# A planner inside a kernel gets a limit of eight transfers in flight, a price for results read on their own engine, later landings, and twelve rounds

## The chip, the core and the metric

The kernel runs on one core of one Trainium2 chip. The metric is the device time of one execution in microseconds; the median of several runs counts.

## The reference

One decoder layer, float32, on 2048 tokens of width 1024. The input projection feeds two groups side by side, a gated causal convolution and an attention without softmax; a shared output projection and a SwiGLU feed-forward block follow.

```python
a = rmsnorm(h, g_pre_mix);  u = a @ W_in        # 1024 -> 512 value | 512 gate | 512 q | 512 k | 512 v
conv_out = silu(layernorm(causal_conv31(u_val * sigmoid(u_gate)) + conv_b))
z = q @ k.T / 8                                 # 8 heads of 64, causal, a token does not see itself
log_beta, log_1m = log_sigmoid(z), log_sigmoid(-z)
A = exp(log_beta + reverse_exclusive_cumsum(log_1m));  attn_out = head_rmsnorm(A @ v)
h = h + rmsnorm(concat(conv_out, attn_out) @ W_out, g_post_mix)
f = (silu(f_in @ W_gate) * (f_in @ W_up)) @ W_down     # f_in = rmsnorm(h, g_pre_ffn), inner width 2816
out = h + rmsnorm(f, g_post_ffn)
```

## The kernel before

TensorE multiplies in a reduced format, so each float32 factor is split into a high part H and a rest L, and a product is made of three matmuls (H by L, H by H, L by H). ScalarE (ACT) rounds a tile to H; VectorE (DVE) or GpSimd (POOL) subtracts to get L. SyncE (SP) issues nearly all transfers.

The tokens are worked in four groups g of 512. For each, `inproj` (L586 to L590, `inps`) makes five kinds of columns for each of four channel blocks c, in the order gate, value, q, k, v. For that it loads a weight tile `raw`, rounds it to `wH` on ACT (L540) and subtracts to `wL` on POOL (L544). Then these run beside each other:

- The convolution, `taps`: 31 taps for each block c, each a multiply-add on DVE (L805, the first L801) that reads what the tap before it wrote, the sum `cv` in PSUM. The last writes `acc`. When a block's taps end, POOL copies the last 30 columns of that block's `glu` to its front (L757), for the next group.
- The attention, `attn`: q and k are split (`qkH` on ACT, `qkL` on DVE, L579), stored to DRAM (`qd`, `kd`, L784 and L785) and loaded again for each head (`QH`, `QL`, `K`, L873 to L880; V like it), since the head layout differs. For each head and each 512 keys there are four blocks of scores: `z` on PE (L892, L893), a mask `msk` added on the diagonal (DVE, L895), two sigmoids on ACT (`om`, `A`), a running product along the keys on DVE (a scan, L902), the product with `A` on POOL (L903), transposes `at` on PE, a split into `TH` and `TL` (ACT, and DVE L579), and the matmuls into `o`.
- The weight sums, `sums`: the feed-forward block is multiplied by Strassen's scheme, which needs sums of weight blocks. For each of them there are a load of `sum` (L1170), an addition on POOL (L1176, 88 in all) and a store `S_...` (L1104), read only after the planned part.

After each group come the output projection (`ops`, L1018 to L1020), a residual addition, and the first feed-forward products (`c11`, `p4`).

All this up to the last output projection is only recorded as it is written. Then `Graph`, a planner inside the kernel, reads the recorded instructions, finds who needs whom, and sets an order on each engine: `forward` runs a list schedule, with a duration for every instruction (`cost`), a latency between engines (`LINK`), and a price for a transfer (AHEAD + bytes / RATE + LAND). `backward` runs it in reverse, to get for each instruction the latest time at which it could start; these times are the priorities of the next `forward`. `arrange` repeats that ROUNDS times and keeps the shortest plan. `in_order` then fixes each engine's order to that plan. The durations and latencies set this order only: on the chip an instruction starts when its engine gets to it and its inputs are there.

In the graph an instruction has two sets of predecessors. Those in `after` must have ended, and the link's latency have passed. Those in `behind` need only have left their engine: the busy time counts, and the latency of the result doesn't. What follows the planned part (the rest of the feed-forward block, `b` and `dps`) keeps its own order.

Of the kernel before, what the change touches and what calls it, by code (L numbers as in the profile page):

```python
# [16 lines left out]
PSUM = bass.MemoryType.PSUM  # L17
# [105 lines left out]
def beside(main, total, sides):  # L123
# [3 lines left out]
    for r in main:  # L127
# [8 lines left out]
        yield r  # L136


RATE, ISSUE, AHEAD, LAND = 350.0, 450.0, 700.0, 2600.0
LINK = {("DVE", "PE"): 57, ("PE", "Activation"): 70, ("Activation", "DVE"): 33, ("Activation", "PE"): 54,  # L140
        ("DVE", "Activation"): 80, ("DVE", "Pool"): 120, ("Activation", "Pool"): 130, ("PE", "DVE"): 37,
        ("Pool", "PE"): 55, ("Pool", "DVE"): 33, ("Pool", "Activation"): 33}
HOP = 60.0
ROUNDS = 8
OVER = (("attn", "late"), ("mixed", "ffnt"), ("psum", "fpsum"))


# [38 lines left out]
def meet(a, b):  # L186
    return a[0] < b[1] and b[0] < a[1] and any(x < w and y < z for x, z in a[2] for y, w in b[2])
# [51 lines left out]
class Graph:  # L239


    def __init__(self, insts):
        self.ops, self.root, self.order, self.users = [], {}, {}, {}
        seen = {}
        for i in insts:
            kind = type(i).__name__
            ins = [a for a in i.ins if hasattr(a, "bass_ap")]
            outs = [a for a in i.outs if hasattr(a, "bass_ap")]
            if not outs:
                continue  # L250
            eng, dma = str(i.engine).split(".")[-1], kind == "InstDMACopy"
            busy, late = (ISSUE, 0) if dma else cost(i, kind, eng, ins, outs)
            o = Op(len(self.ops), i, eng, dma, busy, late, width(outs[0]) * int(outs[0].ap[0][1]) * 4)
            uses = [(a.bass_ap.tensor, box(a), place(a), w) for aps, w in ((ins, False), (outs, True)) for a in aps
                    if hasattr(a.bass_ap.tensor, "tag_meta")]
            for t, b, sp, w in uses:
                if sp != "DRAM" and t.name not in o.tiles:
                    o.tiles.add(t.name)
                    self.users.setdefault(t.name, []).append(o.n)
                    if t.name not in self.root:  # L260
                        self.root[t.name] = t
                        self.order.setdefault(t.tag, []).append(t.name)
                writes, reads = seen.setdefault(t.name, ([], []))
                for q, c in writes + reads if w or sp == "PSUM" else writes:
                    if sp == "PSUM" or meet(b, c):
                        (o.behind if q.eng == eng and not q.dma else o.after).add(q.n)
            for t, b, sp, w in uses:
                writes, reads = seen[t.name]
                if sp == "PSUM":
                    writes[:] = [e for e in writes if e[0].eng != eng] + [(o, b)]  # L270
                elif w:
                    writes[:] = [e for e in writes if not holds(b, e[1])] + [(o, b)]
                    reads[:] = [e for e in reads if not holds(b, e[1])]
                else:
                    reads.append((o, b))
            self.ops.append(o)
        for low, high in OVER:
            under = {o.n for o in self.ops if any(self.pool(x) == low for x in o.tiles)}
            for x in self.root:
                if self.pool(x) == high:  # L280
                    for n in self.roots(x):
                        self.ops[n].after |= {q for q in under if q < n} - self.ops[n].behind
        self.slots()
# [25 lines left out]
    def forward(self, ops, prio, slots=True):  # L309
# [17 lines left out]
        ready = {o.eng: [] for o in ops}  # L327
        busy = dict.fromkeys(ready, 0.0)
        start, stop = [None] * len(ops), [0.0] * len(ops)
        moved = 0.0  # L330
        ev = [(0.0, 0, 0, ())]
        for o in ops:
            if not need[o.n]:
# [28 lines left out]
        while ev:  # L362
# [24 lines left out]
            while look:  # L387
                e = min(look)
                look.remove(e)
                if busy[e] > t + 1e-9:  # L390
                    continue
                while ready[e]:
                    n = heapq.heappop(ready[e])[1]
                    o = ops[n]
                    if slots and not grant(o):
                        continue
                    start[n], busy[e] = t, t + o.busy
                    if o.dma:
                        moved = max(t + AHEAD, moved) + o.size / RATE
                        stop[n] = moved + LAND  # L400
                    else:
                        stop[n] = t + o.late
                    heapq.heappush(ev, (busy[e], 1, n, tuple(iss[n])))
                    for lag, then in fin[n].items():
                        heapq.heappush(ev, (stop[n] + lag, 2, n, tuple(then)))
                    if slots:
                        heapq.heappush(ev, (stop[n] + HOP, 3, n, ()))
                    break
        assert None not in start
        return start, stop, came  # L410

# [1368 lines left out]
```

## Time and profile before

| | |
|---|---|
| three runs | 2518.85, 2523.62, 2527.94 us, median 2523.62 |
| profiled execution | 2518.41 us, its span 2516.7 us |
| PE busy, DVE busy, POOL busy, ACT busy | 2382.0, 1809.7, 1532.1, 1291.9 us |
| mean granted TensorE clock | 0.986 |
| moved by DMA | 657 MB, 261 GB/s on average |

The engines' busy times are sums over the span; PE's matmuls overlap, and its share of 95% says that it is rarely idle and not that it works at its peak. The granted clock is the share of full speed that TensorE got.

### The profile page before, as it was taken

What the parts mean: (1) busy time and instruction counts of PE and PEld (TensorE: products, weight loads), DVE (VectorE), ACT (ScalarE), POOL (GpSimd) and SP (SyncE); (2) the same over time, 40 slices, a digit from 0 to 9 for tenths busy, and PEclk for the clock granted to TensorE, in tenths of its full rate; (3) what the DMA queues carried; (4) which work ended last, traced back from release to release, by engine and by line L of the source; (5) the groups of instructions that cost most, each with busy time, mean ns of one, the idle gap of its engine ahead of it and who ended that gap; (6) DMA issues with size and microseconds to landing.
All of it is one profiled execution on the core that took longest, in us unless ns stands there. A gap on an engine that the chain in (4) does not pass through costs nothing. (4 is left out here: it accounts for less than half of the span.)

```text
span 2516.7 us, 35670 instructions
## 1 busy us (share of the span) xinstructions
PE 2382.0 (95%) x11156; PEld 1933.8 (77%) x11156; DVE 1809.7 (72%) x2321; ACT 1291.9 (51%) x2398; POOL 1532.1 (61%) x1845
## 2 busy tenths in 40 slices
PE   7999987999899999999999998999999999999998
PEld 5777766777688878778778777777788887887886
DVE  5997999769998769997672336776756665557656
ACT  4456656467566655656674655333332234444443
POOL 5666766567575546646962208765666664558656
PEclk9999998999999999999999999999999999999999
DMA  9989886797776879875687786987887868668765
GB/s 325 278 285 345 279 260 203 257 370 243 239 262 213 291 264 323 293 226 173 220 282 260 232 293 228 347 279 246 313 280 273 283 234 277 193 197 264 249 189 179
DMA packets 289181, 657.31 MB, mean 261 GB/s; under 512 B 33888, under 2 KB 42080, under 8 KB 288992
## 3 DMA queue, kind: packets, MB, share of 16 engines
q1 hardware_dynamic: 264704, 622.01, 73.7%
q10 hardware_dynamic: 24288, 33.04, 3.6%
q8 instruction: 88, 1.44, 0.2%
q14 instruction: 101, 0.83, 0.1%
HBM read 460.92 MB, written 193.99 MB: 260 GB/s over the span
## 5 line engine op out<-in xcount | busy, mean ns | idle before, releaser
L903 POOL TENSOR_TENSOR A<-A,om 128x512 f32<-128x512 f32 (+2 forms) x320 | 323.6, 1013 | 317.6 <-DVE om L902 236.5
L1386 POOL TENSOR_TENSOR wL<-raw,wH 128x512 fp32r<-128x512 f32 x176 | 252.8, 1459 | 215.6 <-ACT wH L1385 162.8
L805 DVE SCALAR_TENSOR_TENSOR cv<-glu,cw,cv 128x512 f32<-128x512 f32 x464 | 348.2, 750 | 9.9
L1617 DVE TENSOR_TENSOR xL__22010<-t__22012,xH__22009 128x512 fp32r<-128x512 f32 x154 | 200.7, 1308 | 158.5 <-ACT xH__22009 L1616 158.4
L1615 POOL TENSOR_TENSOR xL__22008<-t__22011,xH__22007 128x512 fp32r<-128x512 f32 x154 | 211.3, 1378 | 156.6 <-ACT xH__22007 L1614 152.6
L902 DVE TENSOR_TENSOR_SCAN om<-om,one,z 128x513 f32<-128x513 f32 (+3 forms) x256 | 277.3, 1096 | 23.9 <-ACT A L900 20.6
L586 PE MATMUL inps<-xH,wL 128*128 128x512 f32 x640 | 259.5, 406 | 6.7 <-POOL wL L544 5.7
L588 PE MATMUL inps<-xH,wH 128*128 128x512 f32 x640 | 256.8, 402 | 0.0
L590 PE MATMUL inps<-xL,wH 128*128 128x512 f32 x640 | 256.1, 401 | 0.0
L579 DVE TENSOR_TENSOR TL<-at,TH 128x512 fp32r<-128x512 f32 (+1 forms) x320 | 186.7, 597 | 85.0 <-ACT TH L578 78.4
L540 ACT ACTIVATE wH<-raw 128x1024 fp32r<-128x1024 f32 x156 | 165.7, 1063 | 159.3 <-PE inps L590 72.9
L1092 PE MATMUL dps<-xH__22007,xL__22010 128*128 128x512 f32 x616 | 240.8, 391 | 4.0 <-DVE xL__22010 L1617 3.1
L1092 PE MATMUL dps<-xL__22008,xH__22009 128*128 128x512 f32 x616 | 240.6, 391 | 1.0 <-POOL xL__22008 L1615 1.0
L1092 PE MATMUL dps<-xH__22007,xH__22009 128*128 128x512 f32 x616 | 240.5, 390 | 0.0
L898 ACT ACTIVATE om<-z 128x512 f32<-128x512 f32 (+2 forms) x320 | 172.7, 540 | 113.6 <-DVE z L895 51.8
L578 ACT ACTIVATE TH<-at 128x512 fp32r<-128x512 f32 (+1 forms) x320 | 167.5, 541 | 80.6 <-PE at L919 64.0
L1614 ACT ACTIVATE xH__22007<-t__22011 128x512 fp32r<-128x512 f32 x154 | 97.3, 632 | 217.0 <-POOL xL__22008 L1615 121.9
L919 PE MATMUL at<-idr,A 128*128 128x128 f32 x1088 | 197.0, 276 | 11.6 <-POOL A L903 7.9
L1385 ACT ACTIVATE wH<-raw 128x512 fp32r<-128x512 f32 x176 | 101.2, 623 | 177.3 <-PE b L1092 57.3
L919 PEld LDWEIGHTS at<-idr,A 128*128 128x128 f32 x1088 | 140.2, 141 | 53.8 <-POOL A L903 12.3
L900 ACT ACTIVATE A<-z 128x512 f32<-128x512 f32 (+2 forms) x320 | 172.4, 544 | 9.6 <-PE at L919 8.7
L892 PE MATMUL z<-K,QL 128*128 128x512 f32 (+2 forms) x320 | 124.9, 393 | 36.8 <-DVE om L902 17.9
(304 smaller groups left out, 6338.8 us busy)
## 6 DMA issues: line engine op xcount, KB each, us to landing
wL<-wL SPq DMA_DIRECT2D x156, 512.0 KB, 5.5
raw<-in_w_in_dram SPq DMA_DIRECT2D x80, 512.0 KB, 5.8
t__22012<-u SPq DMA_DIRECT2D x154, 256.0 KB, 2.8
c<-c ACTq DMA_DIRECT2D x88, 256.0 KB, 5.0
t__22011<-wd SPq DMA_DIRECT2D x88, 256.0 KB, 2.9
K<-kd SPq DMA_DIRECT2D x80, 256.0 KB, 4.7
V<-vd SPq DMA_DIRECT2D x80, 256.0 KB, 4.5
u<-accf SPq DMA_DIRECT2D x22, 768.0 KB, 5.2
```

Of the source, the lines that this page charges most:

```text
L579: nc.vector.tensor_tensor(L, ps, H.bitcast(F32), ALU.subtract)
L586: nc.tensor.matmul(ps, WL[:, kc], aH[t](k), start=k == 0, stop=False)
L588: nc.tensor.matmul(ps, WH[:, kc], aH[t](k), start=False, stop=False)
L590: nc.tensor.matmul(ps, WH[:, kc], aL[t](k), start=False, stop=k == KT - 1)
L805: nc.vector.scalar_tensor_tensor(to, gl[c][:, k:k + G], cw[:, c, k:k + 1], a, ALU.mult, ALU.add)
L902: nc.vector.tensor_tensor_scan(r, r, (one if late else z[:, 0:1]).to_broadcast([P, w + 1]), one, ALU.mult, ALU.bypass)
L903: nc.gpsimd.tensor_tensor(a[:, 0:w], a[:, 0:w], om[:, G - w + 1:G + 1], ALU.mult)
L919: nc.tensor.transpose(pt[:, j * P:(j + 1) * P], u["A"][j][:, b * P:(b + 1) * P], id32)
L1092: return nc.tensor.matmul(ps, a, b, skip_group_check=True, **flags)
L1386: nc.gpsimd.tensor_tensor(l, t, f32(h), sub)
L1615: nc.gpsimd.tensor_tensor(WL, w, f32(WH), sub)
L1617: nc.vector.tensor_tensor(UL, t, f32(UH), sub)
```

## The change

Four edits to the planner; the instructions themselves stay the same.

1. LAND grows from 2600 to 5000 ns, so every planned transfer lands 2.4 us later.
2. At most eight transfers (FLIGHT) are under way at a time: a transfer that would be the ninth is held until the eighth before it has landed. SP then waits; another queue's engine goes on with its other ready instructions.
3. On DVE, ACT and POOL an instruction that reads or overwrites what an earlier one of the same engine wrote moves from `behind` to `after`, with new links of 36, 120 and 70 ns: it may start only when that result has ended and the link has passed. For a tap of 512 columns that is 100 + 36 ns more than before. Reading what an earlier instruction only read, and all of PE's own pairs, stay in `behind`.
4. ROUNDS grows from 8 to 12.

```diff
@@ -136,12 +136,14 @@
         yield r
 
 
-RATE, ISSUE, AHEAD, LAND = 350.0, 450.0, 700.0, 2600.0
+RATE, ISSUE, AHEAD, LAND = 350.0, 450.0, 700.0, 5000.0
 LINK = {("DVE", "PE"): 57, ("PE", "Activation"): 70, ("Activation", "DVE"): 33, ("Activation", "PE"): 54,
         ("DVE", "Activation"): 80, ("DVE", "Pool"): 120, ("Activation", "Pool"): 130, ("PE", "DVE"): 37,
-        ("Pool", "PE"): 55, ("Pool", "DVE"): 33, ("Pool", "Activation"): 33}
+        ("Pool", "PE"): 55, ("Pool", "DVE"): 33, ("Pool", "Activation"): 33, ("DVE", "DVE"): 36,
+        ("Activation", "Activation"): 120, ("Pool", "Pool"): 70}
 HOP = 60.0
-ROUNDS = 8
+FLIGHT = 8
+ROUNDS = 12
 OVER = (("attn", "late"), ("mixed", "ffnt"), ("psum", "fpsum"))
 
 
@@ -261,18 +263,21 @@
                         self.root[t.name] = t
                         self.order.setdefault(t.tag, []).append(t.name)
                 writes, reads = seen.setdefault(t.name, ([], []))
-                for q, c in writes + reads if w or sp == "PSUM" else writes:
-                    if sp == "PSUM" or meet(b, c):
-                        (o.behind if q.eng == eng and not q.dma else o.after).add(q.n)
+                for old, lst in ((True, writes), (False, reads if w else ())):
+                    for q, c, wrote in lst:
+                        if sp == "PSUM" or meet(b, c):
+                            same = q.eng == eng and not q.dma
+                            (o.behind if same and (eng == "PE" or not (old and wrote)) else o.after).add(q.n)
             for t, b, sp, w in uses:
                 writes, reads = seen[t.name]
                 if sp == "PSUM":
-                    writes[:] = [e for e in writes if e[0].eng != eng] + [(o, b)]
+                    writes[:] = [e for e in writes if e[0].eng != eng] + [(o, b, w)]
                 elif w:
-                    writes[:] = [e for e in writes if not holds(b, e[1])] + [(o, b)]
+                    writes[:] = [e for e in writes if not holds(b, e[1])] + [(o, b, True)]
                     reads[:] = [e for e in reads if not holds(b, e[1])]
                 else:
-                    reads.append((o, b))
+                    reads.append((o, b, False))
+            o.behind -= o.after
             self.ops.append(o)
         for low, high in OVER:
             under = {o.n for o in self.ops if any(self.pool(x) == low for x in o.tiles)}
@@ -327,7 +332,7 @@
         ready = {o.eng: [] for o in ops}
         busy = dict.fromkeys(ready, 0.0)
         start, stop = [None] * len(ops), [0.0] * len(ops)
-        moved = 0.0
+        moved, flight = 0.0, []
         ev = [(0.0, 0, 0, ())]
         for o in ops:
             if not need[o.n]:
@@ -389,13 +394,22 @@
                 look.remove(e)
                 if busy[e] > t + 1e-9:
                     continue
+                held = []
                 while ready[e]:
                     n = heapq.heappop(ready[e])[1]
                     o = ops[n]
+                    if o.dma and len(flight) >= FLIGHT and stop[flight[-FLIGHT]] + HOP > t:
+                        held.append((prio[n], n))
+                        if len(held) == 1:
+                            heapq.heappush(ev, (stop[flight[-FLIGHT]] + HOP, 1, n, ()))
+                        if e == "SP":
+                            break
+                        continue
                     if slots and not grant(o):
                         continue
                     start[n], busy[e] = t, t + o.busy
                     if o.dma:
+                        flight.append(n)
                         moved = max(t + AHEAD, moved) + o.size / RATE
                         stop[n] = moved + LAND
                     else:
@@ -406,6 +420,8 @@
                     if slots:
                         heapq.heappush(ev, (stop[n] + HOP, 3, n, ()))
                     break
+                for h in held:
+                    heapq.heappush(ready[e], h)
         assert None not in start
         return start, stop, came
```

The plan moves nearly every instruction of the planned part. Three places show how; the lines after the change count 16 higher, because of the added lines ahead of them.

POOL, early in the first group's projection. Before, one addition of the weight sums and the copy of `glu` stand between the sixth and the seventh weight subtraction:

```order
L522 TENSOR_TENSOR rstd_78<-ms,nhalf 128x1
L544 TENSOR_TENSOR wL<-raw,wH 128x1024 x2
L1176 TENSOR_TENSOR sum<-sum 128x512
L757 COPY glu_137<-glu_137 128x30
L544 TENSOR_TENSOR wL<-raw,wH 128x1024 x2
L1176 TENSOR_TENSOR sum<-sum 128x512
L544 TENSOR_TENSOR wL<-raw,wH 128x1024
```

After, the seventh subtraction stands ahead of the copy, and the additions are gone from here:

```order
L538 TENSOR_TENSOR rstd_78<-ms,nhalf 128x1
L560 TENSOR_TENSOR wL<-raw,wH 128x1024 x3
L773 COPY glu_137<-glu_137 128x30
L560 TENSOR_TENSOR wL<-raw,wH 128x1024
L919 TENSOR_TENSOR A<-A,om 128x128
L921 COPY pv<-om 128x1
L919 TENSOR_TENSOR A<-A,om 128x256
L913 COPY om<-one 128x1
```

So one `wL` moved to the front of the copy, one stayed behind it, and the sums went to later places. Counted over the whole of POOL's order, all 88 sums stood ahead of the 164th of its 320 multiplications by A before; after the change it is 48 of them, and the last stands ahead of the 312th.

DVE, at the end of the second group's projection, around the split of its last k (the second `qkL` of block c = 3). Before, six taps stand in a row ahead of it, and the mask of the z that needs this k comes 9 rows behind it:

```order
L579 TENSOR_TENSOR TL<-at,TH 128x128
L805 SCALAR_TENSOR_TENSOR cv<-glu_139,cw,cv 128x512 x6
L579 TENSOR_TENSOR qkL<-inps,qkH 128x512
L805 SCALAR_TENSOR_TENSOR cv<-glu_139,cw,cv 128x512
L805 SCALAR_TENSOR_TENSOR acc<-glu_139,cw,cv 128x512
L579 TENSOR_TENSOR vt<-vps,vt 128x4x64
L801 TENSOR_SCALAR cv<-glu_141,cw,cbias 128x512
L805 SCALAR_TENSOR_TENSOR cv<-glu_141,cw,cv 128x512 x12
L579 TENSOR_TENSOR vt<-vps,vt 128x4x64
L856 TENSOR_TENSOR xL<-m,xH 128x512
L579 TENSOR_TENSOR TL<-at,TH 128x512
L895 TENSOR_TENSOR z<-z,msk 128x128 x2
```

After, it stands like this, and the mask of the z that needs this k comes 22 rows behind it:

```order
L595 TENSOR_TENSOR TL<-at,TH 128x512
L965 TENSOR_TENSOR ot<-ot,ss_4012 128x512
L595 TENSOR_TENSOR qkL<-inps,qkH 128x512
L821 SCALAR_TENSOR_TENSOR cv<-glu_139,cw,cv 128x512
L911 TENSOR_TENSOR z<-z,msk 128x128
L821 SCALAR_TENSOR_TENSOR cv<-glu_139,cw,cv 128x512
L595 TENSOR_TENSOR TL<-at,TH 128x512
L821 SCALAR_TENSOR_TENSOR cv<-glu_139,cw,cv 128x512 x2
L918 SCALAR_TENSOR_TENSOR om<-om,one,z 128x385
L918 SCALAR_TENSOR_TENSOR om<-om,one,z 128x513
L595 TENSOR_TENSOR TL<-at,TH 128x512 x2
L821 SCALAR_TENSOR_TENSOR cv<-glu_139,cw,cv 128x512
```

The taps are spread between scans and splits of other heads, and more of that attention work lies between `qkL` and the first use of its K.

DVE, in the third group, from the value of block c = 3 on. Before, three runs of taps (5, 8 and 8, the last of them into `acc`) stand ahead of a scan:

```order
L902 SCALAR_TENSOR_TENSOR om<-om,one,z 128x513
L758 TENSOR_TENSOR glu_143<-inps,sg 128x512
L805 SCALAR_TENSOR_TENSOR cv<-glu_139,cw,cv 128x512 x3
L579 TENSOR_TENSOR TL<-at,TH 128x512
L805 SCALAR_TENSOR_TENSOR cv<-glu_139,cw,cv 128x512 x5
L579 TENSOR_TENSOR qkL<-inps,qkH 128x512
L805 SCALAR_TENSOR_TENSOR cv<-glu_139,cw,cv 128x512 x8
L579 TENSOR_TENSOR qkL<-inps,qkH 128x512
L805 SCALAR_TENSOR_TENSOR cv<-glu_139,cw,cv 128x512 x7
L805 SCALAR_TENSOR_TENSOR acc<-glu_139,cw,cv 128x512
L902 SCALAR_TENSOR_TENSOR om<-om,one,z 128x513
```

After, from the same value on:

```order
L774 TENSOR_TENSOR glu_143<-inps,sg 128x512
L821 SCALAR_TENSOR_TENSOR cv<-glu_139,cw,cv 128x512
L595 TENSOR_TENSOR TL<-at,TH 128x512
L821 SCALAR_TENSOR_TENSOR cv<-glu_139,cw,cv 128x512
L918 SCALAR_TENSOR_TENSOR om<-om,one,z 128x513
L821 SCALAR_TENSOR_TENSOR cv<-glu_139,cw,cv 128x512
L595 TENSOR_TENSOR TL<-at,TH 128x512
L821 SCALAR_TENSOR_TENSOR cv<-glu_139,cw,cv 128x512 x2
L918 SCALAR_TENSOR_TENSOR om<-om,one,z 128x513
L821 SCALAR_TENSOR_TENSOR cv<-glu_139,cw,cv 128x512 x2
L918 SCALAR_TENSOR_TENSOR om<-om,one,z 128x513
L821 SCALAR_TENSOR_TENSOR cv<-glu_139,cw,cv 128x512
```

No run of taps is longer than three now, up to five lie between one scan and the next, and this block's taps end later. In all, of 496 taps 291 stood directly behind the tap that they read, and 151 do after the change. On PE the first 216 matmuls and everything behind the planned part keep their order.

## The prediction

> **What bounds the kernel now.** I read the page's head first, then the busy time by stage, then the tensor engine's waits, then the instructions around its three longest waits.
>
> ```profile
> span 2516.7 us, 35670 instructions
> ...
> PE 2382.0 (95%) x11156; PEld 1933.8 (77%) x11156; DVE 1809.7 (72%) x2321; ACT 1291.9 (51%) x2398; POOL 1532.1 (61%) x1845
> ...
> PE   7999987999899999999999998999999999999998
> ...
> PEclk9999998999999999999999999999999999999999
> ```
>
> PE has work for 2382.0 of 2516.7 us, the same matmuls in either kernel. The time to be won is its idle time and the time at a lowered clock. The instructions that the planner orders end near 1512 us, with the last projection:
>
> ```profile
> 1511.82 0.39 PE L1018 MATMUL ops<-wH,e__17074 128*128 128x512 f32 x1
> ```
>
> The windows split there (columns: length, then busy time of PE, PEld, DVE, ACT, POOL, then granted clock, DMA share, GB/s):
>
> ```profile
> 0.00:378.00 378.00, 340.54 (x1677) 273.97 (x1677) 322.75 (x502) 209.10 (x409) 243.93 (x387) 0.98 0.89 295
> 378.00:756.00 378.00, 341.42 (x1656) 272.50 (x1657) 336.76 (x479) 227.26 (x432) 247.26 (x393) 0.96 0.78 262
> 756.00:1134.00 378.00, 365.11 (x1824) 295.73 (x1823) 319.91 (x442) 232.67 (x433) 216.40 (x337) 1.00 0.80 269
> 1134.00:1512.00 378.00, 363.53 (x1744) 294.57 (x1743) 187.24 (x225) 227.38 (x407) 176.69 (x251) 1.00 0.71 242
> 1512.00:2516.00 1004.00, 971.38 (x4259) 797.03 (x4258) 642.99 (x677) 395.46 (x719) 647.80 (x480) 0.99 0.75 253
> ```
>
> PE idles 37.5, 36.6, 12.9 and 14.5 us in the four planned stretches, 101.4 in all, and 32.6 in the unplanned tail, whose PE order is the same in both kernels. So the first 756 us hold the prize: 74 us idle, with DVE at 85 and 89%. What PE waits for there, first up to 400 us and then to 800 (total, times, longest):
>
> ```profile
> PE z L892 <- DMA K<-kd: 17.2, 3, 13.1
> PE tps L596 <- DVE xrow L669: 10.7, 4, 7.5
> PE inps L586 <- POOL wL L544: 5.7, 1, 5.7
> ...
> PE z L892 <- DVE om L902: 12.7, 9, 5.0
> ```
>
> The 10.7 us are the first rows of x; PE's first 216 matmuls keep their order, so they stay. The other three longest waits are the terms of my sum.
>
> **Results read on the same engine.** What does a DVE tap cost when it reads the tap just ahead of it? The first two rows stand where the work alternates, the rest in a chain (start, length):
>
> ```profile
> 299.31 0.75 DVE L805 SCALAR_TENSOR_TENSOR cv<-glu,cw,cv 128x512 f32<-128x512 f32 x1
> 299.97 2.18 DVE L902 TENSOR_TENSOR_SCAN om<-om,one,z 128x385 f32<-128x385 f32 x2
> ...
> 656.37 5.50 DVE L805 SCALAR_TENSOR_TENSOR cv<-glu,cw,cv 128x512 f32<-128x512 f32 x7
> 661.90 0.75 DVE L805 SCALAR_TENSOR_TENSOR acc<-glu,cw,cv 128x512 f32<-128x512 f32 x1
> 662.56 1.28 DVE L902 TENSOR_TENSOR_SCAN om<-om,one,z 128x513 f32<-128x513 f32 x1
> ```
>
> A lone tap frees the engine after 0.66 us (299.97 - 299.31); in the chain one takes 0.79 (5.53 / 7). The old planner put 1.04 x 512 + 108 = 640 ns on each; the new one adds 100 + 36 ns for the next in a chain, 776, which is the measured pace. Of 496 taps, 291 follow their predecessor directly in the old order and 151 in the new: 140 x 0.13 = 18.2 us of DVE time saved. Bounds for PE: none of it (0) to all (-18.2), as DVE is the fuller or the emptier engine at the moment. PE's waits on scans in those 400 us (12.7) are nearest, and chains stand in front of only some of them, so I take a quarter, **-4.5**.
>
> Here the Trainium skill speaks against the change: its page "VectorE: DVE Perf Modes", section "The DRAIN you can't avoid", says that the next DVE operation waits for the pipe to empty anyway and that a semaphore between operations costs nothing extra. By that rule this term would be 0 and the sum 2500 instead of 2496. The trace does not agree: 0.66 against 0.79 us for the same instruction.
>
> **The wait at 659 us.** The z at 663.89 waits for a scan that stands behind 8 + 7 + 1 taps:
>
> ```profile
> 663.89 0.47 PE L892 MATMUL z<-K,QL 128*128 128x128 f32 x1 [4.98 <-DVE om L902]
> ...
> 664.00:672.00 8.00, 7.68 (x28) 5.35 (x28) 7.74 (x16) 3.89 (x11) 5.33 (x13) 0.60 1.05 331
> ```
>
> In the new order the longest run of taps there is three, and the most between two scans five. The 4.98 us go, and with them the lowered clock: 8 us at 0.60 lose 8 x 0.40 = 3.2. **-8.2** (bounds 0 and -8.2). Late next are the taps themselves, which now spread over the following stage; the convolution that they feed is read only after it.
>
> **The wait at 52 us.** POOL, in order, stood before a copy that needs the end of a tap chain (the bracket is its idle time), with two weight subtractions queued behind it:
>
> ```profile
> 55.42 0.21 POOL L757 COPY glu<-glu 128x30 f32<-128x30 f32 x1 [11.45 <-DVE cv L805]
> 55.59 4.68 POOL L544 TENSOR_TENSOR wL<-raw,wH 128x1024 fp32r<-128x1024 f32 x2
> ...
> 58.00 0.80 PE L586 MATMUL inps<-xH,wL 128*128 128x512 f32 x1 [5.67 <-POOL wL L544]
> ...
> 58.00:64.00 6.00, 6.00 (x17) 4.79 (x18) 0.00 (x0) 0.00 (x0) 3.51 (x2) 0.60 0.93 327
> ...
> 49.86 1.05 ACT L540 ACTIVATE wH<-raw 128x1024 fp32r<-128x1024 f32 x1
> ```
>
> Now the seventh subtraction stands ahead of the copy. It can start when its wH ends (50.9) and takes 2.4, so it ends at 53.3 where PE arrives at 52.3: about 1 us is left of 5.67. The eighth stays behind the copy (55.6 + 2.4 = 58.0) and is wanted 24 matmuls later, at about 58.7. With the clock (6 x 0.40 = 2.4): -4.7 - 2.4 = **-7.1** (bounds 0 and -8.1).
>
> **Later landings: the wait at 374 us.** PE waits for a K whose low half DVE finished late, behind a six-tap chain, so that store and load ran in series:
>
> ```profile
> 369.03 4.71 DVE L805 SCALAR_TENSOR_TENSOR cv<-glu,cw,cv 128x512 f32<-128x512 f32 x6
> 373.64 0.68 DVE L579 TENSOR_TENSOR qkL<-inps,qkH 128x512 fp32r<-128x512 f32 x1
> ...
> 374.49 1.23 SPq L785 DMA_DIRECT2D kd<-qkL  x2
> ...
> 378.64 1.19 SPq L880 DMA_DIRECT2D K<-kd  x1
> ...
> 387.10 0.48 PE L892 MATMUL z<-K,QL 128*128 128x128 f32 x1 [13.14 <-DMA K<-kd]
> ...
> DMA to landing us min/median/max: 7.3/7.9/8.4
> ...
> 387.00:392.00 5.00, 4.90 (x21) 4.05 (x22) 3.93 (x8) 2.65 (x8) 1.62 (x7) 0.66 0.91 314
> ```
>
> The old planner let a 256 KB load land after 0.7 + 0.75 + 2.6 = 4.05 us, the new one after 6.45, against 7.9 here. In the new DVE order qkL stands ahead of a good part of the attention work of other heads, 22 rows before the mask of the z that needs this K (9 before), and the z moves back alike. I leave 2 us, since the two other waits for a K total 17.2 - 13.1 = 4.1: -11.1, and -1.7 for the clock (5 x 0.34): **-12.8** (bounds 0 and -14.8).
>
> On the clock the Trainium skill ("TensorE: Matmul & The Clock Gate", section "Why this matters for your kernels") wants no idle gap over about 3 us. The rows above agree for gaps of 5 and more; a 2.56 us gap at 74 us also cost:
>
> ```profile
> 76.66 0.69 PE L892 MATMUL z<-K,QL 128*128 128x384 f32 x1 [2.56 <-DVE om L902]
> ...
> 76.00:80.00 4.00, 3.34 (x11) 2.69 (x11) 3.33 (x8) 2.46 (x6) 3.22 (x4) 0.57 0.91 345
> ```
>
> That page puts the slow spell at about 3.4 us at half speed; three such would be 5.1 us where the rows give 7.3, and the sum 2498.
>
> **Eight in flight, and where the room goes.** At the very start the queue already waits for its own transfers:
>
> ```profile
> SPq L497 <- DMA xrow<-in_x_dram: 2.4, 3, 1.0
> ...
> L1176 POOL TENSOR_TENSOR sum<-sum 128x512 f32<-128x512 f32 x88 | 114.9, 1305 | 58.1 <-DMA sum<-in_w_gate_dram 26.9 <-DMA sum<-in_w_up_dram 20.7 <-DMA K<-kd 9.4
> ```
>
> With the limit in the plan, transfers that nothing waits for soon are put off. These are the weight sums: ahead of the 164th of POOL's 320 A multiplications all 88 stood in the old order (739 us), now 48, and the last stands ahead of the 312th. 40 sums x 1.305 = 52 us of POOL and 80 transfers leave the first half, where POOL itself lost 47.6 us waiting for them. They go where POOL was busy 216 and 177 of 378 us. Only one spot there is full:
>
> ```profile
> 1190.00:1260.00 70.00, 65.25 (x304) 52.14 (x303) 44.46 (x44) 44.77 (x89) 64.26 (x81) 0.98 0.63 215
> ```
>
> Eight sums, 10.4 us, fall among the 22 half-weight subtractions in and around it. Cost between 0 and 10.4; POOL has 5.7 us to spare in 70, so I take **+5**.
>
> **Twelve rounds** only choose among more plans, and cost nothing on the chip. All other waits of the planned part (101.4 - 10.7 - 5.7 - 13.1 - 5.0 = 67 us) are dealt anew: **0**, between -13 (the first half's remaining 40 fall to the second half's 27.4) and +13 (one new wait as long as the longest).
>
> **Sum**: -4.5 - 8.2 - 7.1 - 12.8 + 5 = -27.6 on the profiled execution's 2518.4: 2490.8. The median of the three runs, 2523.6, stands 0.2% above it, so the same gain gives 2496.
>
> **Rivals.** *The whole first half clears up*: both model corrections fit the rows, so its 74 us could fall to the second half's 27.4 plus the 10.7 of the start, -36, and the clock's 0.98 and 0.96 to 1.00, worth up to 22 us, of which about half is idle anyway: -47, 2476. Against it: DVE stays over 80% full. *The waits come back elsewhere*: PE's order is rigid, and a wait removed only lets PE reach the next late result sooner; DVE at 336.76 of 378 us speaks for it. With the three terms halved and +5 unpaid it is -14 + 5, about 2515; with nothing left, 2524. *Slower, by the late sums*: each stands in POOL's row ahead of an A that PE wants. If all 40 lie on PE's path, 52 us against 32.6 won: 2543. It decides from 25 of them (25 x 1.305 = 32.6). Against it: POOL is 47 to 57% busy there.
>
> **Numbers.** My forecast (2484 to 2508) 0.48; cleared first half 0.17; waits partly back (2508 to 2516) 0.12; no change 0.11; slower 0.12. A measurement here tells 0.3%, 7.6 us, from nothing, so faster is 0.48 + 0.17 + 0.12 = 0.77. The range 2470 to 2524 takes in the cleared half and ends at no change; beyond it lie the slower rival and half of no change, 0.18.
>
> **What would show it.** Right: PE idle in the first 756 us near 45; no wait over 3 us at the three places; sums on POOL past 1200 us; single taps between scans. Wrong: a long wait for A on POOL after 756 us, or PE waiting for DVE in the first half as much as now. The untested ground is the 67 us dealt anew.

## The result, and the profile after

The changed kernel takes 2467.39 us in the median of four runs against 2523.65 us; one of the four, of 2633.01 us at a granted clock of 0.849, was disturbed, and the ratio leaves it out (the others took 2463.68, 2464.87 and 2469.91 us). The ratio is 0.9773, with a 95% interval of 0.9745 to 0.98. The prediction was 2496 us, between 2470 and 2524: the sign is right, but the gain is twice as large, 56 us against 28, and the time lies below the range.

The head of the page after (span, busy times, tenths, granted clock):

```profile
span 2461.8 us, 35571 instructions
...
PE 2366.0 (96%) x11156; PEld 1927.0 (78%) x11156; DVE 1805.2 (73%) x2321; ACT 1290.2 (52%) x2398; POOL 1533.3 (62%) x1845
...
PE   8999999998999999999889998999999999999998
...
PEclk9999999999999999999999999999999999999999
```

The last matmul of the planned part, and two windows split there; the third row below is of the kernel before, split at its own end of the planned part:

```profile
1458.57 0.39 PE L1036 MATMUL ops<-wL,e__17073 128*128 128x512 f32 x1
...
0.00:1458.00 1458.00, 1395.76 (x6897) 1130.98 (x6898) 1158.11 (x1644) 893.72 (x1679) 887.43 (x1365) 0.99 0.83 277
1458.00:2460.00 1002.00, 970.24 (x4261) 796.04 (x4259) 647.11 (x677) 396.47 (x720) 645.84 (x480) 1.00 0.75 253
```

```profile
0.00:1512.00 1512.00, 1410.60 (x6898) 1136.77 (x6899) 1166.66 (x1644) 896.41 (x1680) 884.28 (x1366) 0.98 0.80 267
```

The planned part is 54 us shorter and the unplanned tail as long as before (1002 against 1004 us). Of the 54, 39.2 are idle time of PE (1512 - 1410.60 = 101.4 before, 1458 - 1395.76 = 62.2 now). The other 14.8 are busy time of the same 6,900 matmuls, at a mean granted clock of 0.99 instead of 0.98: one per cent of 1400 us. So the gain is what the prediction looked for, idle time and the clock behind it, in the place where it looked. By stage:

```profile
0.00:378.00 378.00, 359.10 (x1819) 293.62 (x1820) 333.02 (x534) 230.36 (x454) 231.93 (x393) 1.00 0.87 282
378.00:756.00 378.00, 363.28 (x1809) 291.58 (x1808) 364.03 (x520) 239.10 (x453) 246.50 (x410) 1.00 0.80 263
756.00:1134.00 378.00, 370.22 (x1849) 301.89 (x1848) 317.24 (x415) 239.02 (x445) 256.52 (x364) 1.00 0.87 297
```

In the first 756 us PE idles 18.9 + 14.7 = 33.6 us (74.0 before), and does 3628 matmuls in the time of 3333. DVE is *fuller* there: 697.1 us busy against 659.5, so its own idle time falls from 96.5 to 59.0. That is the reading to keep. DVE did not become a smaller load; it was waiting for others in the very stretch where it is the fullest engine, and now waits less. What PE waits for in the planned part, up to 1470 us (total, times, longest):

```profile
PE at L935 <- POOL A L919: 9.4, 15, 2.1
PE z L908 <- DVE om L918: 8.7, 13, 1.5
PE tps L612 <- DVE xrow L685: 8.6, 4, 7.4
PE at L935 <- DVE TL L595: 7.4, 6, 2.4
PE o L941 <- DVE TL L595: 5.8, 9, 1.6
PE ops L1034 <- DVE big L1039: 5.5, 3, 3.3
PE c L1108 <- ACT c L1149: 5.2, 3, 2.4
...
PE inps L602 <- POOL wL L560: 1.1, 1, 1.1
```

Three rows of the same view of before, not shown yet:

```profile
PE z L892 <- DVE om L902: 17.9, 15, 5.0
PE o L925 <- DVE TL L579: 11.0, 12, 2.4
...
PE at L919 <- POOL A L903: 7.9, 11, 2.0
```

Waits for K are gone from the list, the longest wait for a scan is 1.5 us (4.98 before), and the one for a weight tile `wL` at the input projection 1.1 (5.67 before). After the start no wait is longer than 3.3 us. DVE at the place of the old 659 us wait shows the new order: a tap stands between almost any two other instructions, and frees the engine after 0.65 to 0.66 us (661.57 to 662.23, 662.83 to 663.48).

```profile
660.97 0.68 DVE L1039 TENSOR_TENSOR big<-ops,big 128x512 f32<-128x512 f32 x1
661.57 0.74 DVE L821 SCALAR_TENSOR_TENSOR cv<-glu,cw,cv 128x512 f32<-128x512 f32 x1
662.23 0.68 DVE L1039 TENSOR_TENSOR big<-ops,big 128x512 f32<-128x512 f32 x1
662.83 0.74 DVE L821 SCALAR_TENSOR_TENSOR cv<-glu,cw,cv 128x512 f32<-128x512 f32 x1
663.48 1.27 DVE L918 TENSOR_TENSOR_SCAN om<-om,one,z 128x513 f32<-128x513 f32 x1
```

### The profile page after: what moved, and what is told of

The parts are those of the page before. It is cut to its first block, busy times and chain, and to the rows that moved or that the text cites. A ratio compares the mean times of both kernels' runs of the same rounds, so it can differ in the third digit from the quotient of the medians.

```text
span 2461.8 us, 35571 instructions
## 1 busy us (share of the span) xinstructions
PE 2366.0 (96%) x11156; PEld 1927.0 (78%) x11156; DVE 1805.2 (73%) x2321; ACT 1290.2 (52%) x2398; POOL 1533.3 (62%) x1845
## 5 line engine op out<-in xcount | busy, mean ns | idle before, releaser
L560 POOL TENSOR_TENSOR wL<-raw,wH 128x1024 fp32r<-128x1024 f32 x50 | 120.4, 2409 | 47.8 <-ACT wH L556 47.1
```

## The experiments

Every kernel is the one before or the one after with other settings of the planner (and one added rule in late_sums, hold_sums and hold_rest). S stands for the same-engine price (the change's third edit, on DVE, ACT and POOL together), F for the limit of transfers and its number, L for LAND at 5000. All ratios are to runs of the kernel before on the same chip.

| kernel | settings | us | ratio (95%) | PE idle, DVE idle in the first 756 us |
|---|---|---|---|---|
| before | none, 8 rounds | 2523.6 | 1 | 74.0, 96.5 |
| same_only | S, 8 rounds | 2506.5 | 0.9941 (0.992 to 0.9962) | 58.9, 113.5 |
| land_only | L, 8 rounds | 2553.0 | 1.012 (1.0093 to 1.0147) | 78.4, 119.8 |
| flight_only | F8, 8 rounds | 2494.7 | 0.9889 (0.9861 to 0.9917) | 57.5, 76.7 |
| rounds_only | 12 rounds | 2526.5 | 1.0016 (1.0002 to 1.0031) | 72.2, 101.7 |
| no_same | L F8, 12 rounds | 2504.2 | 0.9922 (0.9907 to 0.9937) | 48.3, 79.5 |
| no_land | S F8, 12 rounds | 2460.8 | 0.9759 (0.974 to 0.9779) | 36.4, 65.1 |
| no_flight | S L, 12 rounds | 2507.9 | 0.9933 (0.9918 to 0.9948) | 51.4, 87.8 |
| no_rounds | S L F8, 8 rounds | 2469.0 | 0.9785 (0.9769 to 0.9802) | 30.4, 63.8 |
| after | S L F8, 12 rounds | 2467.4 | 0.9773 (0.9745 to 0.98) | 33.6, 59.0 |
| flight16 | S F16, 12 rounds | 2502.0 | 0.992 (0.9898 to 0.9942) | 57.9, 95.5 |
| flight12 | S F12, 12 rounds | 2479.1 | 0.9828 (0.981 to 0.9847) | 46.5, 75.6 |
| flight7 | S F7, 12 rounds | 2468.1 | 0.9781 (0.9764 to 0.9797) | 34.7, 66.5 |
| flight6 | S F6, 12 rounds | 2448.0 | 0.97 (0.9676 to 0.9724) | 26.2, 54.8 |
| flight4 | S F4, 12 rounds | 2519.1 | 0.9988 (0.9975 to 1.0001) | 42.2, 72.2 |
| hold_sums | S, F6 for the weight sums only | 2482.5 | 0.9834 (0.9815 to 0.9852) | 48.7, 82.5 |
| hold_rest | S, F6 for all but the sums | 2458.4 | 0.9746 (0.9725 to 0.9767) | 35.5, 65.0 |
| rate290 | S, RATE 290, 12 rounds | 2541.2 | 1.0066 (1.0047 to 1.0084) | 66.9, 144.0 |
| late_sums | none, sums spread out | 2533.4 | 1.0047 (1.0027 to 1.0067) | 67.2, 97.4 |
| six_late | S L F6, 12 rounds | 2539.3 | 1.0061 (1.0044 to 1.0078) | 44.6, 78.5 |

The idle times come from the first two 378 us windows of each run, as with the rows above. They show where a kernel stands at 756 us and don't rank the kernels: same_only has more DVE idle time than the kernel before and is faster, and flight4 and six_late, well placed here, lose their lead afterwards (below).

### One part alone

Three theories: T1, the price of tap chains made most of it; T2, the transfers (limit and landings) did; T3, a lucky plan, which any edit could have brought.

```diff
 same_only:   keep hunk 3 (same-engine results), undo LAND, FLIGHT, ROUNDS
 land_only:   LAND 2600 -> 5000 alone
 flight_only: the limit of eight alone
 rounds_only: ROUNDS 8 -> 12 alone
```

> The kernel before with one edit alone: results read on the same engine get their price (DVE 36, ACT 120, POOL 70 ns and the result's latency); LAND 2600, no limit in flight, 8 rounds. Directly chained taps fall from 291 to 124, the weight sums stay where they were (all 88 ahead of the 160th A). Theory 1 (the tap chains, priced too low, made most of the first half's waits): 25 to 40 us faster than before, 2484 to 2499, PE idle before 756 us at 40 to 50 us. Theory 2 (the transfers made most: late K and weights, and the sums in the way): at most 15 us faster. Theory 3 (any new plan lands somewhere by luck): anywhere from 20 slower to 40 faster, no better than twelve rounds alone.

> The kernel before with LAND 5000 alone. 77 of the 88 sums stay ahead of the 164th A, chained taps 277. Theory 1: 5 to 12 us faster, since only the wait for K at 374 us goes, and the waits behind taps stay. Theory 2: 15 to 30 faster. Theory 3: within 20 us on either side.

> The kernel before with the limit of eight in flight alone. 76 of the 88 sums stay ahead of the 164th A, chained taps 276. Theory 1: 0 to 8 us faster. Theory 2: 5 to 15 faster, less than with later landings, since the limit binds rarely while a transfer lands in 4 us. Theory 3: within 20 us on either side.

> The kernel before with twelve rounds alone: the planner takes another plan (chained taps 281, sums as before). Theories 1 and 2: within 8 us of before, as the model that chooses is the same. Theory 3: as likely to gain as the other parts, 10 us or more on either side.

The limit is the largest single part (2523.7 x 0.0111 = 28 us), the same-engine price next (15 to 17), the rounds are nothing, and the later landings alone *lose* 30 us. Neither T1 nor T2 had these sizes: the price was to gain 25 to 40 us (T1) or at most 15 (T2), the landings were to gain by both, and the limit was to gain at most 8 (T1) or 15 (T2). T3 allowed 20 us either way for the landings and the limit, and both went beyond it. What the landings do is seen in PE's waits, 0 to 756 us, of land_only:

```profile
PE z L908 <- DVE om L918: 18.9, 12, 7.4
PE o L941 <- DVE TL L595: 17.5, 11, 9.8
PE inps L602 <- POOL wL L560: 9.3, 2, 8.2
```

No z waits for a K any more (before: 17.2 us), which is what was expected of them; but scans, splits and weight tiles come later by more. The landings aren't needed for it either. The same waits, up to 1470 us, of same_only (price alone) and of flight_only (limit alone; the last line of each is the weight tile):

```profile
PE z L908 <- DVE om L918: 17.0, 14, 7.3
PE z L908 <- DMA K<-kd: 7.1, 5, 2.4
...
PE inps L602 <- POOL wL L560: 1.1, 1, 1.1
```

```profile
PE z L908 <- DVE om L918: 7.3, 12, 1.3
...
PE z L908 <- DMA K<-kd: 1.5, 2, 1.0
PE inps L602 <- POOL wL L560: 1.1, 1, 1.1
```

So the price alone shortens the waits for K and for the weight tile, but not those for scans (17.9 us before), though it breaks up more than half of the chained taps (291 to 124); the limit alone shortens all three. Another plan by itself does not: in rounds_only PE still waits 15.6 us for K, 12.7 of them at once.

The price alone, in the first 756 us (same_only, then the kernel before):

```profile
0.00:756.00 756.00, 697.15 (x3361) 557.63 (x3362) 642.53 (x984) 438.55 (x843) 491.31 (x780) 0.96 0.83 279
```

```profile
0.00:756.00 756.00, 681.96 (x3333) 546.47 (x3334) 659.51 (x980) 436.36 (x841) 491.19 (x780) 0.97 0.84 279
```

DVE does nearly the same instructions (984 and 980, of every kind the same count within two) in 17.0 us less, and PE idles 15.1 us less. But PE is only 28 matmuls further at 756 us, some 6 us of work at the row's 0.205 us each (681.96 / 3333), since its busy time rose too, at a clock of 0.96 against 0.97. The planned part ends 18 us earlier, so about 12 of them are won after 756 us.

### One part taken out

Here T1 says that limit and landings together do most, T2 that the chain price does most once the transfers are planned soundly, T3 again luck.

```diff
 no_same:   the changed kernel without hunk 3
 no_land:   the changed kernel with LAND 2600
 no_flight: the changed kernel without a limit
 no_rounds: the changed kernel with ROUNDS 8
```

> The changed kernel without the price for results on the same engine; chained taps are back at 276, the weight sums stay late (43 of 88 ahead of the 164th A). Theory 1 (limit and landings together do most, since with the limit the plan stops filling the queue with sums): 30 to 40 us faster than before, about 2488. Theory 2 (the chain price does most, with sound transfers behind it): at most 10 us faster. Theory 3 (luck of the plan): anywhere from 2480 to 2550.

> The changed kernel with LAND 2600: limit, chain price and twelve rounds stay; 72 of the 88 sums ahead of the 164th A. Adding the two parts as measured alone gives -28 - 17 = -45, 2478. Theory 1: less than the whole change by 10 to 20 us, 2478 to 2488, since late sums and early loads need the later landing under a limit. Theory 2: as good as the whole change, within 6 us of 2467. Theory 3: 2460 to 2520.

> The changed kernel without the limit in flight; 75 of the 88 sums ahead of the 164th A. Later landings alone were 30 us slower than before, the chain price alone 17 faster. Theory 1: later landings without a limit make the plan issue earlier what the queue then can't carry, so this stays slow: 2520 to 2545. Theory 2: 2490 to 2505. Theory 3: anywhere from 2470 to 2550.

> The changed kernel with 8 rounds; another plan, but chained taps 132 and late sums (47 ahead of the 164th A) as in the whole change. Theories 1 and 2: within 10 us of 2467. Theory 3: 20 us or more from it as likely as not.

Without the limit 40 us go, without the price 37, without the landings none (the kernel is 7 us faster). T1 and T2 are both off again: no_same gains 20 us over the kernel before, where T1 said 30 to 40 and T2 at most 10, and no_flight lies 3 us above T2's band; only no_land is where T2 had it. At the old landing the limit and the price gain 28 and 17 us alone and 63 together (no_land); at the later landing 49 (land_only to no_same) and 45 (land_only to no_flight) alone and 86 together. So they add up, and the runs do not show that they help each other beyond that: the surplus of 18 us at the old landing turns into a lack of 8 at the later one. A lucky plan (T3) doesn't explain this: the six kernels with S and a limit of six to twelve for all transfers (six_late, below, apart) lie between 2448 and 2479 us, and of the others only hold_rest is below 2482.

### How tight, and by way of the sums?

A: eight stands near what the chip carries. B: any limit keeps transfers that nobody waits for out of the queue. C: the limit helps by putting off the weight sums.

```diff
 flight12, flight6, flight16: no_land with FLIGHT = 12, 6, 16
 late_sums: the kernel before, and in Graph:
+        for k, o in enumerate(loads):           # the 88 loads of weight sums
+            o.after.add(muls[min(int(k * 3.5), 307)].n)   # POOL's multiplications by A
```

> All parts of the change except the later landings, with a limit of twelve transfers under way instead of eight. Its neighbours: 2460.8 us with eight, about 2505 us with no limit (the same-engine price alone, 2506.5). Theory A (eight stands near what the chip really carries, and a plan that lets more go is wrong about it): the gain shrinks steadily with the limit, so 2470 to 2480 us here and more at sixteen. Rival B (any limit that keeps transfers nobody waits for out of the queue does it): 2458 to 2468 us. Rival C (the limit helps through the weight sums, which it puts off): the plan here has 83 of 88 sums ahead of the 164th multiplication by A against 72 with eight, so nearly all of the gain goes, 2490 to 2505 us. K waits in the first half (17.2 us in the kernel before, 2.2 with eight): A 5 to 10 us, B under 4 us.

> The same with a limit of six. A: fewer than the chip carries, so transfers are planned later than need be, 2465 to 2475 us, with more waits of POOL and PE for weight tiles. B: 2458 to 2468 us, until six starves the weight loads. C: 57 sums ahead of the 164th multiplication by A, fewer than with eight, so as fast as eight or faster, 2450 to 2461 us.

> The same with a limit of sixteen. A: most of the gain gone, 2485 to 2500 us. B: 2458 to 2470 us still. C: 84 of 88 sums ahead of the 164th multiplication by A, so 2490 to 2505 us.

> The kernel before with one thing added to its planner: the load of the k-th weight sum may start only after the 3.5k-th multiplication by A, which spreads the sums evenly over the planned part (45 of 88 ahead of the 164th multiplication by A, as in the changed kernel, against 87 before). No limit, no new price, old landings, eight rounds. A and B: the sums are not what the limit moves to advantage, 2515 to 2532 us. C: the sums in the first half took POOL's time and the transfers' that the projection needed, so 15 to 28 us faster, 2495 to 2508 us.

From sixteen to six the time falls by 54 us, in steps of 23, 18 and 13; flight6 is the fastest kernel of this study, 72 us below the runs of the kernel before beside it (2520.2). C falls: the sums spread out by themselves gain nothing (ratio 1.0047), and six is faster than C's band. B falls, since sixteen has hardly a gain. Of A, the steady shrinking holds from eight up (twelve in its band, sixteen 2 us above it), but not that eight is best. Two rows each of same_only (no limit) and flight6 (0 to 378 and 378 to 756 us) show how it acts:

```profile
0.00:378.00 378.00, 345.09 (x1684) 277.58 (x1685) 308.57 (x502) 210.17 (x413) 245.19 (x386) 0.97 0.90 299
378.00:756.00 378.00, 352.06 (x1679) 280.05 (x1678) 333.96 (x483) 228.38 (x430) 246.12 (x394) 0.95 0.77 259
```

```profile
0.00:378.00 378.00, 363.60 (x1857) 300.02 (x1858) 342.48 (x548) 235.54 (x464) 247.28 (x407) 1.00 0.87 292
378.00:756.00 378.00, 366.24 (x1834) 294.80 (x1833) 358.75 (x515) 244.79 (x465) 261.17 (x428) 1.00 0.83 280
```

DVE's idle time falls from 113.5 to 54.8 us and PE's from 58.9 to 26.2, while the transfers move as much (279 and 286 GB/s on average). The largest group of loads doesn't land sooner either: the loads of `raw` in the first 756 us of the kernel before, and of flight6:

```profile
DMA to landing us min/median/max: 3.6/5.9/9.0
```

```profile
DMA to landing us min/median/max: 3.5/5.8/9.0
```

So, as far as these loads show, the limit is no relief of a crowded queue on the chip. It changes in which order things are planned.

### Which transfers, the rate, and too tight

D: only the sums must be held back. E: transfers of all kinds cost when planned too early. F: the limit merely repairs a rate that the plan takes too high.

```diff
 hold_sums, hold_rest: no_land with FLIGHT = 6, and
-                    if o.dma and len(flight) >= FLIGHT and ...
+                    if o.dma and is_sum(o) and len(flight) >= FLIGHT and ...    # hold_rest: not is_sum(o)
-                        if e == "SP":
-                            break
 rate290: no_land without a limit, RATE 350 -> 290
 flight4: no_land with FLIGHT = 4
```

> Same-engine price, old landings, twelve rounds, and a limit of six that holds back only the loads and stores of the weight sums; every other transfer goes as if there were no limit. Neighbours: 2448 us with six for all, 2506 us with no limit. Theory D (the sums are what must not stand ahead of urgent transfers in the queue): most of the gain, 2445 to 2465 us. Theory E (all kinds of transfers issued too early cost): less than half of it, 2480 to 2505 us. Theory F (the wrong rate): nothing is put right, 2500 us.

> The same limit of six on all transfers except those of the weight sums. All 88 sums stand ahead of the 164th multiplication by A here, as in the kernel before. D: the sums go freely and take the places of the held ones, so little gain or a loss, 2495 to 2525 us. E: half of the gain or more, 2455 to 2480 us.

> Same-engine price, old landings, twelve rounds, no limit, and the plan's rate of transfers at 290 bytes per ns instead of 350, near the 279 GB/s that the trace shows in the first 756 us. F: the plan sees its backlog at its true length and the gain comes without a limit, 2450 to 2475 us. D and E: the backlog stays unlimited and only grows in the plan, 2495 to 2515 us.

> A limit of four for all transfers, otherwise as with six (2448 us). Only 35 of 88 sums stand ahead of the 164th multiplication by A, and four in flight at a plan's latency of 3.3 us plus their length let about 1 us pass for each 256 KB, a rate of some 260 GB/s, below what the first half moved before. If the tight limit starves the projection: 2465 to 2500 us, with waits of PE for weight tiles. If only the queue's depth counts: 2435 to 2450 us.

Both hold kernels differ from the limit for all in one thing more: SP goes on with other transfers where it would wait. E holds: against same_only (2506.5, with eight rounds, which rounds_only and no_rounds show to matter by 3 us at most) the limit on everything but the sums gains 48 us, on the sums alone 24, on all 58.5. In hold_rest all 88 sums stand as early as in the kernel before, so putting them off isn't needed. F fails: with a rate near the measured one the plan is 35 us slower, where F said a gain and D and E no change, and DVE idles 144.0 us. Making transfers look slower in the plan lost 30 us by the landing alone and 35 by the rate beside the price (the landing beside the price lost nothing, no_flight against same_only); making it choose late gained. Four is too tight, and slower than both its bands (2435 to 2450, 2465 to 2500). Its first 378 us move 251 GB/s and keep POOL busy for 216.81 us, against 292 and 247.28 with six; here are these and the stages after 756 us:

```profile
0.00:378.00 378.00, 354.10 (x1754) 287.81 (x1755) 330.29 (x526) 222.92 (x435) 216.81 (x367) 0.99 0.78 251
...
756.00:1134.00 378.00, 356.79 (x1754) 286.83 (x1753) 303.07 (x416) 224.22 (x420) 228.39 (x337) 0.98 0.81 274
1134.00:1430.00 296.00, 276.10 (x1315) 222.09 (x1314) 150.07 (x165) 169.62 (x312) 194.48 (x242) 0.98 0.78 266
```

That is only a part of its loss. At 756 us flight4 has done 3519 matmuls, 186 more than the kernel before; from there to 1430 us it does 3069 against 3225, and what follows the planned part takes 12 us longer. Its weight sums have moved far back: 48 of the 88 additions on POOL start after 756 us, the last at 1496.5 us (739.0 before), POOL idles 54.7 us there until their loads land, and PE waits for weight splits on POOL:

```profile
PE p L1108 <- POOL wL L573: 10.7, 7, 3.0
...
PE c L1108 <- POOL wL L560: 6.0, 3, 2.9
```

### Luck, and six with the later landings

```diff
 flight7:  no_land with FLIGHT = 7
 six_late: the changed kernel with FLIGHT = 6
```

> Same-engine price, old landings, twelve rounds, a limit of seven. Its neighbours are 2460.8 us with eight and 2448 us with six. If the limit itself sets the time and plans differ little by luck: 2446 to 2463 us. If luck of a plan is 10 us or more, it may fall outside. Here 122 taps stand right behind another tap on DVE, against 141 with eight and 144 with six, so a theory by which the broken tap chains are what gains has it below both, under 2446 us.

> The changed kernel with a limit of six in place of eight: later landings (5000 ns), same-engine price, twelve rounds. With six transfers of 256 KB under way in a plan whose latency is 5.7 us plus their length, the plan moves some 240 GB/s, less than the first half moved before (279 GB/s). Only 35 sums stand ahead of the 164th multiplication by A, and 209 taps behind another tap, as in the limit of four at early landings (35 sums, 2519 us). If the two settings act through the plan's total rate: 2485 to 2520 us, a loss against eight. If six is better whatever the landing: 2440 to 2460 us.

flight7 misses its band by 5 us: it is slower than both neighbours, 2468 against 2461 and 2448. So a single plan can be some 10 us off the trend, and differences of that size between settings (six and eight, or the 7 us of no_land over the changed kernel) can't be put down to the setting. The tap chains don't set it either: flight7 has the fewest taps behind another tap, 122, and is the slowest of the three. six_late is slower still than four with the early landings (2539 against 2519 us, and above the 2485 to 2520 expected if the plan's total rate counts), and its first row has the same 250 GB/s and 210.76 us of POOL. The total rate is one reading of that; late sums are another. At 756 us six_late is 205 matmuls ahead of the kernel before, and it loses them afterwards with 49 sums past 756 us, the last at 1511.2. No run separates the two.

```profile
0.00:378.00 378.00, 344.11 (x1703) 278.70 (x1703) 321.77 (x516) 212.87 (x418) 210.76 (x360) 0.98 0.79 250
```

## Why the prediction was right or wrong

- **Where the time is.** Right: the prize was PE's idle time in the first 756 us and the lowered clock. It fell to 33.6 us, where 45 was forecast.
- **Results read on the same engine, -4.5.** Too small, and by another path than the one named. The lone tap's 0.66 us stands again in the new trace, and the price alone takes 17.0 us of DVE's time out of the first half; but that is for 167 chained taps fewer, where the 18.2 was worked out for 140 over the whole planned part. In the changed kernel DVE's busy time in the planned part falls by only 8.5 us (1166.66 to 1158.11), as some other rows of DVE take longer there (the 24 splits `xL` of `xcol` 26.3 us instead of 19.5). The failed step is the quarter, which was taken from the waits for scans: with the price alone these stay at 17.0 us, the waits for K and for the weight tile fall from 17.2 to 7.1 and from 5.7 to 1.1 us, and the run is 15 to 17 us shorter. The row on DVE (85 and 89% busy beside an idle PE) should have outweighed the 12.7 us of waits for scans: late scans are not the only way in which a full engine holds up others. The price also covers pairs on ACT and POOL, and no run has DVE's alone. The Trainium skill's page "VectorE: DVE Perf Modes", section "The DRAIN you can't avoid", was taken to make this term nothing; the section adds that an operation which isn't held starts earlier, and 0.66 against 0.79 us agrees with that sentence.
- **The waits at 659 and 52 us, -8.2 and -7.1.** Right in size as far as the trace shows: what is left at these lines is at most 1.5 and 1.1 us. The cause named for the first isn't shown: same_only breaks the chains and still has a wait of 7.3 us for a scan, and with the limit alone the longest is 1.3.
- **Later landings, -12.8.** The wait for K did go, and the longer price does remove it (land_only); but crediting the edit with it was wrong, since the price on results or the limit alone brings it down to 7.1 or 1.5 us as well. The landing costs 30 us alone, by the waits for scans, splits and weight tiles that it brings, and no_land, without it, is no slower. The step looked at one wait that the price would cure, and not at the plan in which every transfer has it.
- **Eight in flight, +5.** This step failed most. Its sign is wrong: the limit gains 28 us alone and 40 (no_flight) beside the other edits. I saw only what it puts off, the sums, and charged POOL for it. A charge on that path hardly shows: PE's waits for A on POOL are 9.4 us in the planned part, against 7.9. The rival "slower, by the late sums" does not come true here, where the last sum starts at 1302.1 us; flight4 and six_late, with sums up to 1496.5 and 1511.2, look more like it.
- **The other 67 us, 0.** They fell as well, to about 52 (62.2 idle, less 8.6 for the first rows of x and 1.1 for the weight tile): waits for `om` go from 17.9 to 8.7 us and for `TL` at `o` from 11.0 to 5.8. With the terms of the price and the limit the forecast had +0.5 us here and the traces have about -14; that and the clock below are most of the 27 us that the forecast lacks. The rival "the whole first half clears up" (2476) came nearest in number, partly by luck: its argument was that both model corrections, the same-engine price and the landing, fit the rows, and these two without the limit gain 16 us (no_flight). Holding DVE's fullness against it was an error all the same, as DVE had 96.5 us of idle time there to give.
- **Twelve rounds, 0.** Right: 1.0016, and 2467.4 against 2469.0 us.
- **The clock.** Three places gave 7.3 us; the 14.8 us of busy time that went are about twice that, so shorter gaps, which the sum left out, probably cost clock too. The Trainium skill ("TensorE: Matmul & The Clock Gate", section "Why this matters for your kernels") warns of idle gaps over about 3 us; the trace agrees as far as it goes, with one wait over 3 us left after the start (3.3) and a clock of 0.99 in the planned part; but before, a gap of 2.56 us was followed by 4 us at 0.57 too.

**What stays open.** Shown is that the limit acts through the order, on weights, q, k and v more than on the sums, that it gains from sixteen down to six (eight to six within a plan's luck), and that with it DVE and PE idle less in the first half. The price gains in every pair of runs, but by which pairs of which engine isn't shown. Not shown is the step inside the planner. The diff suggests one: a held transfer goes back among the ready ones, so that a more urgent one which becomes ready meanwhile passes it, where without a limit it would stand in the plan's queue already. No run isolates that from the buffers that an early transfer occupies. Nor is it shown why four, or six with the later landings, loses after 756 us: the late sums stand there, but so does everything else that is planned later.

## What to carry to other kernels

When a planner's model is corrected, price the plan as a whole: the correction that fits one measured wait best (here the landing) may lose, and a rule that only delays decisions may gain most. Look at the idle time of the fullest engine beside the one that bounds: 96 us of it in DVE's fullest stretch said that the order could still improve; but look at the later stages too, as a better first half is lost again in flight4 and six_late. Try such a limit at several values, and take steps of 10 us between neighbouring plans for luck.

## What was not expected of the hardware

Nothing in the runs contradicts the rows used before. Two things are worth a number: the landing times of the `raw` loads hardly changed with the limit (a median of 5.9 and 5.8 us for 512 KB), although the planned queue was cut to six; and a tap that follows another instruction frees DVE after 0.66 us in the new trace too, against 0.79 behind a tap, which in the first 756 us of same_only came to 17 us of DVE time.
